# A streaming-encoder block on one core: the order of the two input norms' pieces in the engines' queues

## Chip, cores, metric

The kernel runs on 1 core of one Trainium2 chip. The metric is the device time of one execution in microseconds. A program on one core keeps five engines busy side by side: TensorE (PE, matmuls; PEld is its weight load), VectorE (DVE), ScalarE (ACT), GpSimd (POOL) and SyncE (SP, here only transfers). Each works off its own queue in order; an instruction that waits holds back everything behind it on its engine.

## The reference, cut to what matters

One layer on 512 tokens, with 16 learned meta tokens put in front (528 rows of 1024). The layer norms the rows, projects them to all branches at once, runs stick-breaking attention and gated linear attention, gates and adds both, adds the normed result to the input, and applies a gated MLP with a causal convolution, again normed on both sides:

```python
def _rmsnorm(x, g):
    xf = x.astype(jnp.float32)
    y = xf * lax.rsqrt(jnp.mean(xf * xf, axis=-1, keepdims=True) + EPS)
    return (y * g.astype(jnp.float32)).astype(x.dtype)

h = jnp.concatenate([meta, x], axis=1)
...
    hn = _rmsnorm(h, norm_mix_pre[l])            # the first norm
    proj = hn_p @ w_in[l]
    sb_q, sb_k, sb_v, g_q, g_k, g_v, g_r, g_lr, merge = _split_cols(proj, IN_WIDTHS)
    ...                                          # the two attention branches
    mix = (gate_sb * (sb @ w_sb_out[l]) + gate_gla * (o @ w_gla_out[l])) @ w_o[l]
    h = h + _rmsnorm(mix, norm_mix_post[l])      # the second norm: this one,
    hn = _rmsnorm(h, norm_ffn_pre[l])            # and this one behind it
    up = hn @ w_ffn_up[l]
    act = jax.nn.gelu(_causal_dwconv(up, conv_w[l], conv_b[l]), approximate=True)
    ffn = (act * (hn @ w_ffn_gate[l])) @ w_ffn_down[l]
    h = h + _rmsnorm(ffn, norm_ffn_post[l])
return h[:, N_META:]
```

## The kernel before

All matmul operands are split in two: a high part, the value rounded to a shorter format (a cast on ScalarE), and a low part, the rest (a subtraction on VectorE or GpSimd). A product is three matmuls: high by high, high by low, low by high. `load_w` (L79) loads a weight block `raw`, casts it to `wh` and subtracts to `wl`; `proj` (L100) runs the matmuls of one block of 128 output columns over up to two segments of tokens, `ALL` = 0 to 272 (meta tokens and tiles 1 and 2) and 272 to 528 (tiles 3 and 4). With `by_part` it takes all high-by-high matmuls first, then those with `wl`, then those with the input's low part.

**The order of the queues.** The kernel is traced as a sequence of operations, and a planner puts each engine's instructions in an order of its own: it simulates the program, and an engine takes what is ready by the simulated times, earlier-traced work first. A block under `with tc.issue_after(ins)` binds its instructions on the engine of `ins` behind `ins`. A tile with one buffer (`bufs=1`) is handed on only when its last reader is done, so instructions that write such tiles follow each other.

**First norm** (pool `p0`, L214 on). Four tiles of 128 tokens, `xts[1..4]`, and the meta tokens as one 128x128 tile `xm`. `stats(i)` squares and sums a tile on ScalarE and calls `rstd_of`, which gets 1/sqrt as exp(-ln/2) on ScalarE and refines it in three small steps on VectorE (L127, L132, L136; the last gives the factor). `scaled` applies the factor, `turned(i, r)` transposes on TensorE (`tp`, or `tpm` for the meta tokens) and calls `split_g`: gain on VectorE (`yg`, L210), cast to `hnh` on ScalarE (L211), low part `hnl` on the engine in the table `LO` (L212). The trace order is: tiles 1 and 2, the weights of the first block `gk` (columns C_GK) with its low part on VectorE, the loads of tiles 3 and 4, the meta tokens, some warming matmuls (`warm`), and the first half of the gk projection (`only=[0]`, tokens 0 to 272). Then come tiles 3 and 4, two rank-16 projections `lr` (L393), and in `gla_proj` the second half of gk.

**Second norm** (pool `pw`, L848 on). `second(i)` is the output projection of tile i for the right 512 columns (`wob`), `first_half(i, ...)` for the left (`wo`). `gained(i, pt, hf)` squares a half on ScalarE (`wj`, L863) and applies the gain on VectorE (`hb`, L864). `normed(i)` takes the factor over both halves (`whole`, L868), adds the input (L881), squares each half of the sum on ScalarE (`wk`, L883), takes the next factor and writes `y` (L888). `turned(i, b)` transposes half of y (`ht`, L897), casts it to `h2h` on ScalarE and subtracts to `h2l` on VectorE (L142, L143). The two meta tokens that the convolution needs go through `mini`, in three parts. All squares write one scratch tile `junk` with one buffer; the tiles of `rstd_of` have one buffer in this pool, too. The first two blocks of the MLP's up and gate projections (`up`, `ga`) are run for tiles 1 and 2 first, with the transposes of tiles 3 and 4 in between, and then for tiles 3, 4 and the meta columns.

Of the kernel before, what the change touches and what calls it, by code (L numbers as in the profile page):

```python
# [16 lines left out]
P = 128  # L17
# [32 lines left out]
def block_kernel(ctx: ExitStack, tc: tile.TileContext, x, meta_tokens, norm_mix_pre, w_in, w_gk_up, b_gk,  # L50
# [28 lines left out]
    def load_w(src, nk, name, hi_out=None, lo_out=None, lo_eng=pool, into=None):  # L79

        ncol = src.shape[-1]
        raw = wp.tile([P, nk, ncol], F32, tag="raw", name=f"raw_{name}")
        sp.dma_start(raw, src)
        last_raw[0] = raw
        if hi_out is None:
            hi_out = (into or wp).tile([P, nk, ncol], F32R, tag="wh", name=f"wh_{name}", bufs=2)
            lo_out = (into or wp).tile([P, nk, ncol], F32R, tag="wl", name=f"wl_{name}", bufs=2)
        act.copy(hi_out, raw)  # L88
        lo_eng.tensor_tensor(out=lo_out, in0=raw, in1=f32(hi_out), op=ALU.subtract)  # L89
        return hi_out, lo_out  # L90
# [26 lines left out]

    last_exp = [None]

    def rstd_of(pl, ss, n, name, between=None, rest=None):  # L120

        shp = list(ss.shape)
        r0 = pl.tile(shp, F32, tag=f"rs_r{shp[1]}", name=f"r0_{name}")
        act.activation(r0, ss, AF.Ln, scale=1.0 / n, bias=rest[0] if rest else epst[: shp[0]])
        last_exp[0] = act.activation(r0, r0, AF.Exp, scale=-0.5)
        v = pl.tile(shp, F32, tag=f"rs_v{shp[1]}", name=f"v_{name}")
        dve.tensor_scalar(out=v, in0=ss, scalar1=-0.5 / n, scalar2=rest[1] if rest else -0.5 * EPS, op0=ALU.mult, op1=ALU.add)  # L127
        if between:
            between()
        a = pl.tile(shp, F32, tag=f"rs_a{shp[1]}", name=f"a_{name}")  # L130
        if shp[1] == 1:
            dve.tensor_scalar(out=a, in0=v, scalar1=r0, scalar2=r0, op0=ALU.mult, op1=ALU.mult)  # L132
        else:
            dve.tensor_tensor(out=a, in0=r0, in1=r0, op=ALU.mult)
            dve.tensor_tensor(out=a, in0=a, in1=v, op=ALU.mult)
        dve.scalar_tensor_tensor(out=a, in0=a, scalar=1.5, in1=r0, op0=ALU.add, op1=ALU.mult)  # L136
        return a
# [69 lines left out]
    def split_g(pl, hi, lo, src, g, nm, lo_eng=dve):  # L207

        y = pl.tile([P, *src.shape[1:]], F32, tag="yg", name=f"yg{nm}", bufs=4)
        last_yg[0] = dve.tensor_tensor(out=y, in0=src, in1=g.unsqueeze(2).broadcast_to(list(src.shape)), op=ALU.mult)  # L210
        last_hi[0] = act.copy(hi, y)  # L211
        return lo_eng.tensor_tensor(out=lo, in0=y, in1=f32(hi), op=ALU.subtract)  # L212

    with tc.tile_pool(name="p0", bufs=2, side="right") as p0:  # L214
# [37 lines left out]
        def scaled(xt, r, eng):  # L252

            if eng is act:
                act.mul(xt, xt, r)
            else:
                eng.tensor_scalar(out=xt, in0=xt, scalar1=r, scalar2=None, op0=ALU.mult)

        def turned(i, r):
            if not i:  # L260
                tp = pst("tpm")
                last_tp[0] = pe.transpose(tp[:, :P], xm, ident)
                split_g(p0, hnh[:, :, :NM], hnl[:, :, :NM], tp[:, :P].rearrange("p (t k) -> p k t", k=KT), gT, "m")
                return
            t = slice(NM + (i - 1) * P, NM + i * P)
            for b in range(2):
                scaled(xts[i][:, 512 * b : 512 * b + 512], r, SC[i][b])
            for b in range(2):
                tp = pst(f"tp{i}_{b}", "sz"[i % 2])
                for k in range(4):  # L270
                    c = (4 * b + k) * P
                    with tc.issue_after(last_pr[0].ins) if i > 2 else ExitStack():
                        last_tp[0] = pe.transpose(tp[:, k * P : (k + 1) * P], xts[i][:, c : c + P], ident)
                ks = slice(4 * b, 4 * b + 4)
                low = split_g(p0, hnh[:, ks, t], hnl[:, ks, t], tp.rearrange("p (k t) -> p k t", k=4), gT[:, ks], f"{i}_{b}", LO[i][b])
            return low

        last_tp = [None]
        SC = {1: (dve, dve), 2: (act, dve), 3: (dve, dve), 4: (act, act)}
        LO = {1: (pool, pool), 2: (dve, pool), 3: (dve, pool), 4: (dve, pool)}  # L280
        d1 = stats(1)
        d2 = stats(2, last_exp[0])
        turned(1, d1)
        d0 = stats(0, last_exp[0])
        scaled(xm, d0, act)
        low2 = turned(2, d2)
        with tc.issue_after(last_exp[0].ins), tc.issue_after(last_yg[0].ins):
            first = {"k": load_w(cols(w_in, C_GK), KT, "gk0", lo_eng=dve)}
        for i in (3, 4):
            sp.dma_start(xts[i], x[(i - 1) * P : i * P, :])  # L290
        rlr = cst.tile([P, KT, RANK], F32, name="rlr")
        sp.dma_start(rlr, cols(w_in, C_LR, RANK))
        turned(0, d0)
        hi2 = last_hi[0]
        with tc.issue_after(last_tp[0].ins):
# [3 lines left out]
        d4 = stats(4, last_exp[0])  # L299
        turned(3, d3)  # L300
        low4 = turned(4, d4)

# [42 lines left out]
    with ExitStack() as pgs:  # L345
# [22 lines left out]
        with tc.tile_pool(name="plr", bufs=2) as plr:  # L368
# [20 lines left out]
            for lo, hi in ALL:  # L389
# [4 lines left out]
                if not lo:  # L394
                    first["lr"] = last_lr
                act.copy(gst[0:RANK, lo:hi], lr[0:RANK])
                act.copy(gst[64 : 64 + RANK, lo:hi], lr[0:RANK])
# [13 lines left out]
        def gla_proj(h):  # L411
            r = []
            for nm, c0, sc in (("k", C_GK + h * P, 1.0), ("q", C_GQ + h * P, GK ** -0.5)):
                w = first[nm] if h == 0 else load_w(cols(w_in, c0), KT, f"g{nm}{h}")
                if h == 0 and nm == "k":
                    pt = first["pt"]
                    proj(w, hnh, hnl, ALL, f"g{nm}{h}", only=[1], pt=pt)
                    pt = pt[:, 512 - 272 : 768]
# [429 lines left out]
    with tc.tile_pool(name="pw", bufs=1) as pw:  # L848
# [7 lines left out]
        sq2 = pw.tile([P, 5, 2], F32, name="sq2")  # L856

        def gained(i, pt, hf):
# [4 lines left out]
            act.activation(junk, pt, AF.Square, accum_out=sq[:, i, hf : hf + 1])  # L863
            dve.tensor_tensor(out=hb[:, i - 1, c], in0=pt, in1=g1bc[:, c], op=ALU.mult)  # L864
# [5 lines left out]

        last_tr = [None]

        ys = {}

        def normed(i):

            h, xi = hb[:, i - 1, :], xr[:, i - 1, :]
            r = whole(i, sq, "mix")
            for hf in range(2):
                c = slice(hf * 512, hf * 512 + 512)  # L880
                dve.scalar_tensor_tensor(out=h[:, c], in0=h[:, c], scalar=r, in1=xi[:, c], op0=ALU.mult, op1=ALU.add)  # L881
                junk = pw.tile([P, 512], F32, tag="junk", name=f"wk{i}_{hf}")
                act.activation(junk, h[:, c], AF.Square, accum_out=sq2[:, i, hf : hf + 1])  # L883
            r = whole(i, sq2, "ffn")
# [5 lines left out]
        def turned(i, b):  # L890
# [7 lines left out]
            ks = slice(4 * b, 4 * b + 4)  # L898
            split(h2h[:, ks, t], h2l[:, ks, t], tp.rearrange("p (k t) -> p k t", k=4))
            last_tr[0] = last_ht  # L900
# [90 lines left out]
        gained(3, second(3, {11: lambda: turned(1, 0), 17: lambda: turned(1, 1)}), 1)  # L991
        normed(3)
        m = mini()
        next(m)
        gained(4, second(4, {5: lambda: turned(2, 0), 11: lambda: turned(2, 1), 17: lambda: next(m)}), 1)
        normed(4)
        gas = [load_w(cols(w_gate, m * P), KT, f"ga{m}", into=wx) for m in range(2)]
# [264 lines left out]
```

## Time and profile before

| | |
|---|---|
| median of 3 runs | 939.47 us (938.93 to 939.78) |
| profiled execution | 938.61 us, of which the span of its instructions 936.9 us |
| busy in the span | PE 915.9 us (98%), PEld 839.4, DVE 621.9 (66%), ACT 494.2 (53%), POOL 355.6 (38%) |
| granted TensorE clock, mean | 0.992 |
| DMA | 93.38 MB, mean 100 GB/s |

Rows of instructions in order of time read: start in the span, duration of the group, engine, line of the kernel, operation, written tile <- read tiles, shape, count; in brackets the engine's idle time ahead of it and what ended it. Rows of a stretch give its length, the busy time of each engine with its number of instructions, the granted clock, and the DMA share and rate. Small groups of the same kind are merged into one row.

### The profile page before, as it was taken

The page shows a single profiled execution, that of the slowest core. Times are in us where ns is not written, and L with a number is a line of the kernel's source. Part 1 is how long each engine was busy: PE and PEld are TensorE (multiplying, and loading weights), DVE is VectorE, ACT ScalarE, POOL GpSimd, SP SyncE. Part 2 cuts the span into 40 slices and gives each one's busy share as a digit, 9 for nine tenths or more (in the row PEclk, how much of TensorE's full clock was granted, in tenths as well). Part 3 has the DMA queues.
Part 4 walks back from the last instruction along what each step waited for, and adds up shares of the span by engine and source line. Part 5 has one row for each costly group of instructions (what it writes and reads, how often), then busy time and mean ns, then how long its engine had stood idle before and what let it go on. Part 6 is the DMA issues. An engine that isn't in the chain of part 4 may idle for free.

```text
span 936.9 us, 17749 instructions
## 1 busy us (share of the span) xinstructions
PE 915.9 (98%) x7156; PEld 839.4 (90%) x7156; DVE 621.9 (66%) x1072; ACT 494.2 (53%) x938; POOL 355.6 (38%) x259
## 2 busy tenths in 40 slices
PE   7999999999999999999999998999999999999997
PEld 7999999999999998989998687999999999988885
DVE  6585858686559786888647357455554444578997
ACT  7674747575567665766754245433333333355654
POOL 6533332323355453555545322544444444200200
PEclk9999999999999999999999998999999999999999
DMA  7222222222222222222224542333333333264933
GB/s 203 66 70 75 63 68 69 69 69 69 69 68 69 68 66 72 68 69 68 57 79 127 211 135 90 108 96 91 90 91 90 93 100 100 91 232 184 239 113 131
DMA packets 129875, 93.38 MB, mean 100 GB/s; under 512 B 4080, under 2 KB 114930, under 8 KB 129794
## 3 DMA queue, kind: packets, MB, share of 16 engines
q1 hardware_dynamic: 126178, 82.55, 29.6%
q10 hardware_dynamic: 2112, 6.82, 1.9%
q0 software_dynamic: 1504, 2.88, 1.8%
q8 instruction: 56, 0.92, 0.4%
q14 instruction: 25, 0.20, 0.1%
HBM read 88.05 MB, written 4.19 MB: 98 GB/s over the span
## 4 chain that ended last, share of the span: by engine, by line
PE 94%; DVE 2%; ACT 2%; issue 1%; DMA 0%; POOL 0%; DVEq 0%; POOLq 0%; ACTq 0%
PE pt_up L115 14%; PE ga L936 13%; PE pt_gr L115 5%; PE pt_gv L115 5%; PE pt_mg L115 5%; PE pt_ms L115 5%; PE pt_go L115 5%; PE dA L1108 3%; PE dB L1108 3%; PE dD L1108 3%; PE pt_sv L115 3%; PE pt_gk L115 3%; PE pt_so L115 3%; PE wob L951 3%; PE pt_sk L115 3%; PE pt_gq L115 2%
## 5 line engine op out<-in xcount | busy, mean ns | idle before, releaser
L89 POOL TENSOR_TENSOR wl_up<-raw_up,wh_up 128x1024 fp32r<-128x1024 f32 x22 | 52.9, 2407 | 82.4 <-ACT wh_up L88 82.4
L89 POOL TENSOR_TENSOR wl_ga<-raw_ga,wh_ga 128x1024 fp32r<-128x1024 f32 x22 | 55.3, 2518 | 74.8 <-ACT wh_ga L88 57.5
L115 PE MATMUL pt_up<-h2h,wh_up 128*128 128x256 f32 (+1 forms) x352 | 74.7, 287 | 1.3 <-ACT h2h L142 1.3
L115 PE MATMUL pt_up<-h2l,wh_up 128*128 128x256 f32 (+1 forms) x352 | 74.6, 286 | 0.0
L115 PE MATMUL pt_up<-h2h,wl_up 128*128 128x256 f32 (+1 forms) x352 | 74.4, 285 | 0.0
L936 PE MATMUL ga<-h2h,wh_ga 128*128 128x512 f32 (+1 forms) x192 | 72.5, 377 | 0.0
L936 PE MATMUL ga<-h2h,wl_ga 128*128 128x512 f32 (+1 forms) x192 | 72.3, 377 | 0.0
L936 PE MATMUL ga<-h2l,wh_ga 128*128 128x512 f32 (+1 forms) x192 | 72.3, 377 | 0.0
L88 ACT CAST wh_up<-raw_up 128x1024 fp32r<-128x1024 f32 x22 | 23.1, 1049 | 79.3 <-PE pt_up L115 76.4
L115 PEld LDWEIGHTS pt_up<-h2h,wh_up 128*128 128x128 f32 x352 | 58.0, 193 | 3.5 <-ACT h2h L142 1.8
L115 PEld LDWEIGHTS pt_up<-h2l,wh_up 128*128 128x128 f32 x352 | 56.6, 193 | 0.0
L115 PEld LDWEIGHTS pt_up<-h2h,wl_up 128*128 128x128 f32 x352 | 56.5, 192 | 0.0
L936 PEld LDWEIGHTS ga<-h2h,wl_ga 128*128 128x128 f32 x192 | 36.4, 190 | 7.0
L936 PEld LDWEIGHTS ga<-h2h,wh_ga 128*128 128x128 f32 x192 | 36.7, 191 | 6.1
L936 PEld LDWEIGHTS ga<-h2l,wh_ga 128*128 128x128 f32 x192 | 36.4, 190 | 6.2
L1039 DVE SCALAR_TENSOR_TENSOR cy<-pt_up,cw,cy 128x511 f32<-128x511 f32 (+1 forms) x22 | 16.4, 745 | 36.7 <-ACT cy L1036 36.7
L88 ACT CAST wh_ga<-raw_ga 128x1024 fp32r<-128x1024 f32 x22 | 23.1, 1048 | 26.8 <-PE ga L936 25.6
L1039 DVE SCALAR_TENSOR_TENSOR yp<-pt_up,cw,yp 128x511 f32<-128x511 f32 (+1 forms) x22 | 16.4, 745 | 30.9 <-ACT yp L1036 30.9
L1136 POOL DMA_DIRECT2D tv<-in_w_ffn_down_dram x6 | 7.0, 1172 | 68.4 <-DVE wl_p L143 68.4
L89 POOL TENSOR_TENSOR wl_gr<-raw_gr,wh_gr 128x1024 fp32r<-128x1024 f32 x8 | 19.1, 2385 | 31.0 <-ACT wh_gr L88 29.5
L142 ACT CAST sh_p<-As 128x512 fp32r<-128x512 f32 (+1 forms) x30 | 17.3, 584 | 23.9 <-PE dB L1108 9.6
L115 PE MATMUL pt_gr<-hnh,wh_gr 128*128 128x258 f32 (+1 forms) x128 | 28.2, 294 | 0.0
(574 smaller groups left out, 3140.9 us busy)
## 6 DMA issues: line engine op xcount, KB each, us to landing
raw_up<-in_w_ffn_up_dram SPq DMA_DIRECT2D x22, 512.0 KB, 3.9
raw_ga<-in_w_ffn_gate_dram SPq DMA_DIRECT2D x22, 512.0 KB, 3.8
raw_t<-in_w_ffn_down_dram SPq DMA_DIRECT2D x10, 512.0 KB, 7.4
raw_gv<-in_w_in_dram SPq DMA_DIRECT2D x8, 512.0 KB, 3.9
raw_gr<-in_w_in_dram SPq DMA_DIRECT2D x8, 512.0 KB, 3.8
raw_mg<-in_w_in_dram SPq DMA_DIRECT2D x8, 512.0 KB, 3.9
raw_go<-in_w_gla_out_dram SPq DMA_DIRECT2D x8, 512.0 KB, 4.2
raw_ms<-in_w_in_dram SPq DMA_DIRECT2D x8, 512.0 KB, 3.8
```

What stands on the lines that cost most here:

```text
L88: act.copy(hi_out, raw)
L89: lo_eng.tensor_tensor(out=lo_out, in0=raw, in1=f32(hi_out), op=ALU.subtract)
L115: last_pr[0] = pe.matmul(dst, a[:, k, :], b[:, k, lo:hi], start=n == 0, stop=n == len(steps) - 1)
L142: act.copy(hi, src)
L936: last_mm[0] = pe.matmul(pt[:, lo:hi], a[:, k, :], b[:, k, lo:hi], start=lo == 0 and k == 0 and q == 0, stop=k == KT - 1 and q == 2, skip_ ...
L951: last_mm[0] = pe.matmul(pt, a, b, start=q == 0, stop=q == len(ops) - 1)
L1039: dve.scalar_tensor_tensor(out=y[:, d:], in0=pt[:, : SEQ - d], scalar=c, in1=y[:, d:], op0=ALU.mult, op1=ALU.add)
L1108: mm[i] = pe.matmul(dsts[i], a, b, start=first and k == 0 and j == 0, stop=last and k == NP - 1 and j == 2, skip_group_check=True)
L1136: return lambda n, q, nk: pool.dma_start(out=t[:, q : q + nk, :], in_=block(s, c, q, nk), accum_op=ALU.add)
```

## The change

In the first norm the order of the trace and the bindings are changed. `turned` only scales and transposes; `split_g` and the table move to `parted`. The gain of tile 2's second half is bound behind the meta tokens' factor `r0`; the casts of tile 1's second half and of tile 2 are bound behind the scaling of `xm`. The low parts of tile 1's second half and tile 2 and of the meta tokens all run on VectorE, behind the low part of gk's weights and one behind the other; before, GpSimd had both of tile 1 and the second of tile 2. The transpose of the meta tokens takes a buffer of the other PSUM tag. The loads of tiles 3 and 4 come after that in the trace. The second half of the gk projection moves to directly behind the first `lr` product, in the order of `by_part`.

In the second norm the first factors of tiles 3 and 4 are taken together, after tile 4's first square and ahead of both `normed`; tile 3's second squares are bound behind tile 4's first, and the casts of tile 3's transposes behind tile 4's last square.

```diff
@@ load_w, split_g: lo_eng=None leaves the low part to the caller
+        if lo_eng is None:
+            return raw, hi_out, lo_out
...
+        if lo_eng is None:
+            return lambda: dve.tensor_tensor(out=lo, in0=y, in1=f32(hi), op=ALU.subtract)
@@ first norm
-        LO = {1: (pool, pool), 2: (dve, pool), 3: (dve, pool), 4: (dve, pool)}
+        LO = {1: (pool, None), 2: (None, None), 3: (dve, pool), 4: (dve, pool)}
+        first = {}
         d1 = stats(1)
         d2 = stats(2, last_exp[0])
-        turned(1, d1)
+        t1 = turned(1, d1)
+        parted(1, 0, t1[0])
         d0 = stats(0, last_exp[0])
-        scaled(xm, d0, act)
-        low2 = turned(2, d2)
-        with tc.issue_after(last_exp[0].ins), tc.issue_after(last_yg[0].ins):
-            first = {"k": load_w(cols(w_in, C_GK), KT, "gk0", lo_eng=dve)}
+        r0 = last_r[0]
+        t2 = turned(2, d2)
+        with tc.issue_after(last_exp[0].ins):
+            raw, *first["k"] = load_w(cols(w_in, C_GK), KT, "gk0", lo_eng=None)
+        xs = scaled(xm, d0, act)
+        tp = pst("tpm", "z")
+        last_tp[0] = pe.transpose(tp[:, :P], xm, ident)
+        with tc.issue_after(xs.ins):
+            low11 = parted(1, 1, t1[1])
+        with tc.issue_after(xs.ins):
+            low20 = parted(2, 0, t2[0])
+        with tc.issue_after(r0.ins):
+            low21 = parted(2, 1, t2[1])
+        with tc.issue_after(last_yg[0].ins):
+            lowm = split_g(p0, hnh[:, :, :NM], hnl[:, :, :NM], tp[:, :P].rearrange("p (t k) -> p k t", k=KT), gT, "m", None)
+        hi2 = last_hi[0]
+
+        with tc.issue_after(last_yg[0].ins):
+            low = dve.tensor_tensor(out=first["k"][1], in0=raw, in1=f32(first["k"][0]), op=ALU.subtract)
+        with tc.issue_after(low.ins):
+            last = low20()
+        for f in (lowm, low11, low21):
+            with tc.issue_after(last.ins):
+                last = f()
         for i in (3, 4):
             sp.dma_start(xts[i], x[(i - 1) * P : i * P, :])
...
-        turned(0, d0)
-        hi2 = last_hi[0]
@@ rank projections and gla_proj
                 if not lo:
                     first["lr"] = last_lr
+                    proj(first["k"], hnh, hnl, ALL, "gk0", only=[1], pt=first["pt"], by_part=True)
...
-                    proj(w, hnh, hnl, ALL, f"g{nm}{h}", only=[1], pt=pt)
@@ second norm
-            act.activation(junk, pt, AF.Square, accum_out=sq[:, i, hf : hf + 1])
+            last_wj[0] = act.activation(junk, pt, AF.Square, accum_out=sq[:, i, hf : hf + 1])
...
-                act.activation(junk, h[:, c], AF.Square, accum_out=sq2[:, i, hf : hf + 1])
+                with tc.issue_after(last_wj[0].ins) if i == 3 else ExitStack():
+                    last_wk[0] = act.activation(junk, h[:, c], AF.Square, accum_out=sq2[:, i, hf : hf + 1])
...
-            split(h2h[:, ks, t], h2l[:, ks, t], tp.rearrange("p (k t) -> p k t", k=4))
+            with tc.issue_after(last_wk[0].ins) if i == 3 else ExitStack():
+                split(h2h[:, ks, t], h2l[:, ks, t], tp.rearrange("p (k t) -> p k t", k=4))
...
-        normed(3)
         m = mini()
         next(m)
         gained(4, second(4, {5: lambda: turned(2, 0), 11: lambda: turned(2, 1), 17: lambda: next(m)}), 1)
-        normed(4)
+        rs = [whole(i, sq, "mix") for i in (3, 4)]
+        normed(3, rs[0])
+        normed(4, rs[1])
```

More of the change, by code (lines that the diff above doesn't have):

```diff
@@ L118, in block_kernel @@
     last_exp = [None]
+    last_r = [None]
     def rstd_of(pl, ss, n, name, between=None, rest=None):
@@ L135, in rstd_of @@
             dve.tensor_tensor(out=a, in0=a, in1=v, op=ALU.mult)
-        dve.scalar_tensor_tensor(out=a, in0=a, scalar=1.5, in1=r0, op0=ALU.add, op1=ALU.mult)
+        last_r[0] = dve.scalar_tensor_tensor(out=a, in0=a, scalar=1.5, in1=r0, op0=ALU.add, op1=ALU.mult)
         return a
@@ L254, in scaled @@
             if eng is act:
-                act.mul(xt, xt, r)
-            else:
-                eng.tensor_scalar(out=xt, in0=xt, scalar1=r, scalar2=None, op0=ALU.mult)
+                return act.mul(xt, xt, r)
+            return eng.tensor_scalar(out=xt, in0=xt, scalar1=r, scalar2=None, op0=ALU.mult)
         def turned(i, r):
[L260 to L265, printed above, removed]
             for b in range(2):
                 scaled(xts[i][:, 512 * b : 512 * b + 512], r, SC[i][b])
+            tps = []
             for b in range(2):
-                tp = pst(f"tp{i}_{b}", "sz"[i % 2])
+                tps.append(pst(f"tp{i}_{b}", "sz"[i % 2]))
                 for k in range(4):
@@ L272, in turned @@
                     with tc.issue_after(last_pr[0].ins) if i > 2 else ExitStack():
[L273 to L276, printed above, removed]
+                        last_tp[0] = pe.transpose(tps[b][:, k * P : (k + 1) * P], xts[i][:, c : c + P], ident)
@@ L278, in block_kernel, with parted @@
+            return tps
+        def parted(i, b, tp):
+            t, ks = slice(NM + (i - 1) * P, NM + i * P), slice(4 * b, 4 * b + 4)
+            return split_g(p0, hnh[:, ks, t], hnl[:, ks, t], tp.rearrange("p (k t) -> p k t", k=4), gT[:, ks], f"{i}_{b}", LO[i][b])
         last_tp = [None]
         SC = {1: (dve, dve), 2: (act, dve), 3: (dve, dve), 4: (act, act)}
-        LO = {1: (pool, pool), 2: (dve, pool), 3: (dve, pool), 4: (dve, pool)}
+        LO = {1: (pool, None), 2: (None, None), 3: (dve, pool), 4: (dve, pool)}
@@ L299, in block_kernel @@
         d4 = stats(4, last_exp[0])
-        turned(3, d3)
-        low4 = turned(4, d4)
+        for i, d in ((3, d3), (4, d4)):
+            for b, tp in enumerate(turned(i, d)):
+                low4 = parted(i, b, tp)
         cr = p0.tile([FT, 4, P], F32, name="cr", bufs=1)
@@ L856, in block_kernel @@
         sq2 = pw.tile([P, 5, 2], F32, name="sq2")
+        last_wj = [None]
         def gained(i, pt, hf):
@@ L871, in block_kernel, with normed @@
         last_tr = [None]
+        last_wk = [None]
         ys = {}
-        def normed(i):
+        def normed(i, r=None):
             h, xi = hb[:, i - 1, :], xr[:, i - 1, :]
-            r = whole(i, sq, "mix")
+            r = whole(i, sq, "mix") if r is None else r
             for hf in range(2):
```

## The prediction, made before the run

> **What bounds the kernel now.** I read the shares by engine first, then the chain that ended last, then TensorE's waits, then the granted clock in stretches, and last the instructions in order of time around the two norms.
>
> ```profile
> PE 94%; DVE 2%; ACT 2%; issue 1%; DMA 0%; POOL 0%; DVEq 0%; POOLq 0%; ACTq 0%
> ```
>
> The chain is TensorE nearly throughout. So a change pays only where TensorE stands idle or slow, and what it saves there moves everything behind it. TensorE's waits name the places; the longest (total, times, longest) lies in the second norm, and one of 2.24 in the first (in brackets behind tpm, further down):
>
> ```profile
> PE ht L897 <- DVE y L888: 2.6, 1, 2.6
> ```
>
> A wait has an aftermath. The next rows are stretches of 3.41 us; their columns are length, busy PE, PEld, DVE, ACT, POOL, then the granted clock:
>
> ```profile
> 13.96:17.37 3.41, 3.41 (x17) 3.38 (x16) 2.23 (x7) 2.71 (x7) 1.54 (x1) 0.50 0.98 237
> 249.48:252.89 3.41, 3.41 (x20) 3.34 (x19) 0.12 (x1) 1.74 (x7) 2.29 (x1) 0.50 0.01 2
> 563.51:566.92 3.41, 1.86 (x14) 1.57 (x14) 2.68 (x4) 2.42 (x5) 3.41 (x2) 1.00 0.20 58
> 566.92:570.33 3.41, 3.41 (x19) 3.41 (x18) 3.31 (x13) 1.72 (x6) 0.31 (x1) 0.50 0.88 247
> 583.99:587.40 3.41, 3.41 (x17) 3.41 (x18) 1.23 (x2) 0.54 (x1) 0.00 (x0) 0.50 0.03 5
> ```
>
> After a stretch in which TensorE stood 1.55 us (563.51: 3.41 - 1.86), the next 3.41 us ran at clock 0.50, though TensorE was busy throughout. At half the rate such a stretch costs 3.41/2 = 1.7 us. The four slow stretches start a multiple of 3.413 us apart (235.52 = 69 of them, 317.44 = 93, 17.07 = 5), so they lie on a grid in time.
>
> **First norm.** ScalarE, then VectorE, then GpSimd, then TensorE, each in order of time (start, duration, engine, line, what):
>
> ```profile
> 10.05 1.03 ACT L88 CAST wh_gk<-raw_gk 128x1024 fp32r<-128x1024 f32 x1
> 10.99 1.65 ACT L211 CAST hnh<-yg 128x512 fp32r<-128x512 f32 x3
> 12.55 0.40 ACT L255 ACTIVATE xm<-xm,a_in 128x128 f32<-128x128 f32 x1
> 14.60 0.30 ACT L211 CAST hnh<-ygm 128x128 fp32r<-128x128 f32 x1 [1.65 <-DVE ygm L210]
> ```
>
> ```profile
> 10.57 0.26 DVE L132 TENSOR_SCALAR a_in<-v_in,r_in 128x1 f32<-128x1 f32 x1
> 10.80 0.69 DVE L210 TENSOR_TENSOR yg<-tp,gT 128x512 f32<-128x512 f32 x1
> 11.40 0.15 DVE L136 SCALAR_TENSOR_TENSOR a_in<-a_in,r_in 128x1 f32<-128x1 f32 x1
> 11.47 1.22 DVE L89 TENSOR_TENSOR wl_gk<-raw_gk,wh_gk 128x1024 fp32r<-128x1024 f32 x1
> 12.61 1.76 DVE L212 TENSOR_TENSOR hnl<-yg,hnh 128x512 fp32r<-128x512 f32 x1
> 14.29 0.28 DVE L210 TENSOR_TENSOR ygm<-tpm,gT 128x128 f32<-128x128 f32 x1
> ```
>
> ```profile
> 11.68 3.82 POOL L212 TENSOR_TENSOR hnl<-yg,hnh 128x512 fp32r<-128x512 f32 x2 [0.28 <-ACT hnh L211]
> ```
>
> ```profile
> 13.00 0.33 PE L262 MATMUL tpm<-ident,xm 128*128 128x128 f32 x1 [2.24 <-ACT xm L255]
> 13.16 2.05 PE L228 MATMUL warm<-ident 128*128 128x128 f32 x12
> 14.95 2.18 PE L115 MATMUL pt_gk<-hnh,wh_gk 128*128 128x272 f32 x8
> 16.93 1.36 PE L115 MATMUL pt_gk<-hnh,wl_gk 128*128 128x272 f32 x8
> 18.13 0.41 PE L115 MATMUL pt_gk<-hnl,wh_gk 128*128 128x272 f32 x2
> ```
>
> The first projection starts at 14.95, and the meta tokens set that: their factor is split by a gain of tile 2 (10.80 between 10.57 and 11.40), their scaling waits behind three casts (10.99 to 12.55), and their gain waits behind a low part that takes 1.76 while GpSimd subtracts too.
>
> After the change, step by step. (1) The gain at 10.80 is bound behind the factor, which then ends at 10.57 + 0.26 + 0.15 = about 11.02. (2) The three casts are bound behind the scaling, which starts when wh_gk ends (11.08) and ends at 11.48. (3) The transpose starts at 11.55, the twelve warming matmuls behind it; in the row 14.95 - 13.00 = 1.95 us pass from transpose to projection, so the projection can start at 13.50. (4) VectorE: the moved gain runs 11.05 to 11.74, ygm 12.0 to 12.3. (5) ScalarE: the three casts 11.48 to 13.1, the meta cast to 13.4, in time for 13.50. The gain is 14.95 - 13.50 = 1.45 us.
>
> What is moved lands on VectorE: low parts of tile 1's and tile 2's second halves leave GpSimd, and wl_gk now waits for ygm, with four low parts in a fixed order behind it. GpSimd keeps one subtraction, ahead of them, so I price a 512-wide low part at 0.69, not 1.76, from this later row:
>
> ```profile
> 26.32 0.69 DVE L212 TENSOR_TENSOR hnl<-yg,hnh 128x512 fp32r<-128x512 f32 x1
> ```
>
> From 12.3: 1.22 + 3 x 0.69 + 0.3 (128 wide, as ygm) = 15.9. wl_gk is there at 13.5 and first wanted 1.98 us after the start (16.93 - 14.95), at 15.5; the low parts 3.18 us after it (18.13 - 14.95), at 16.7. So they are hidden with 0.8 to spare at the slow clock. Without that cover (a fast clock wants them at 13.50 + 16 x 0.125 = 15.5) they cost 0.4. If they ran at 1.76 each they would end at 19.1 and cost 2.4: the bounds are 0 and 2.4, and I take 0, since the row of a VectorE alone is the near one. Tiles 3 and 4 follow the last meta cast through ScalarE, which starts their squares as much sooner. SP's transfers keep their order, but now stand in the trace behind the casts of gk; those for tiles 3 and 4 wait for no result, and I count nothing.
>
> The second half of the gk projection is moved ahead, between the two rank projections, and taken in the order high, low weight, low input. TensorE does the same matmuls, so the price is 0 unless it then meets a low part that is not there (the 26.32 row is the last of them): between a loss of 2.2 us and no effect; I take 0.
>
> **Second norm.** ScalarE, VectorE, TensorE:
>
> ```profile
> 571.17 0.60 ACT L863 ACTIVATE wj<-wob 128x512 f32<-128x512 f32 x1
> ...
> 575.88 0.63 ACT L883 ACTIVATE wk<-hb 128x512 f32<-128x512 f32 x1 [2.23 <-DVE hb L881]
> 576.42 0.18 ACT L883 ACTIVATION_READ_ACCUMULATOR wk<-hb 128x1 f32 x1
> 578.13 0.59 ACT L142 CAST h2h<-ht 128x512 fp32r<-128x512 f32 x1 [1.53 <-PE ht L897]
> 578.14 0.33 ACTq L1009 DMA_DIRECT2D hbd<-hb  x1
> 578.62 0.63 ACT L883 ACTIVATE wk<-hb 128x512 f32<-128x512 f32 x1
> ```
>
> ```profile
> 574.59 0.28 DVE L132 TENSOR_SCALAR a_mix<-v_mix,r_mix 128x1 f32<-128x1 f32 x1
> 574.90 0.16 DVE L136 SCALAR_TENSOR_TENSOR a_mix<-a_mix,r_mix 128x1 f32<-128x1 f32 x1
> 575.09 1.41 DVE L881 SCALAR_TENSOR_TENSOR hb<-hb,a_mix,xr 128x512 f32<-128x512 f32 x2
> ...
> 581.71 1.41 DVE L888 SCALAR_TENSOR_TENSOR y<-hb,a_ffn,g2bc 128x512 f32<-128x512 f32 x2
> 583.04 0.17 DVE L143 TENSOR_TENSOR h2l<-hmg,h2h 128x16 fp32r<-128x16 f32 x1
> ```
>
> ```profile
> 582.52 1.38 PE L897 MATMUL ht<-ident,y 128*128 128x128 f32 x8 [2.56 <-DVE y L888]
> ```
>
> The last tile's second half was ready at 576.5 (575.09 + 1.41), but its square stood behind a cast that waited 1.53 for a transpose, and ran at 578.62. y followed at 581.71, and TensorE stood 2.56. The change binds that cast behind the square: 2.1 us (578.62 - 576.5) by itself. It also takes tile 4's first square (571.17) ahead of tile 3's second ones, and both first factors ahead of both tiles. The factor's tile has one buffer, so tile 4's factor still waits until tile 3's hb is done; but it no longer waits for tile 3's y. y moves by the stretch between: a y pair (1.41) and the two or three small steps around it (0.28, 0.16 each), some 2 us more. Of 4.1 us TensorE needs 2.56. So the wait goes, and the slow stretch after it (1.7) has no cause.
>
> What is late next: TensorE goes from the transposes straight to the second halves, which need the casts of tile 4 (0.59 each) and the meta columns, whose low part came at 583.04, behind y. With y gone from there I take 0.3 us of new waiting; the bounds are 0 and 2.56 (all of it given back). In front, tile 4's first square (0.60) may now stand before a cast of tile 2, which TensorE waits for (part of the 1.55 in the stretch from 563.51): 0 to 0.6, and I take 0, since the casts come first in the trace. Gain: 2.56 + 1.7 - 0.3 = 3.96 us.
>
> The Trainium skill, "TensorE: Matmul & The Clock Gate", section "HAM oscillation — how this bites in real kernels", gives as its rule that gaps above about 3.4 us are to be avoided. The trace differs: 1.55 us in one stretch was enough. By that rule a gap of 2.56 would leave the clock alone, and the sum would lose its 1.7. The same page (Part 1) says the window is free-running and does not reset with the kernel; the grid of 3.413 agrees, and no run here shows whether its phase repeats.
>
> **Sum.** 1.45 + 3.96 = 5.4 us. The profiled execution took 938.61 (span 936.9 and 1.7 around it), 0.86 under the median of 939.47. 938.61 - 5.4 = 933.2, beside that median 934.1.
>
> **Rivals.**
> *More slow stretches go.* The gap in front of the first projection shrinks by 1.45, and the others shift on the grid; 249.48 and 566.92 follow gaps only just long enough to slow a stretch. Against: in the first norm tiles 3 and 4 are then bound by ScalarE, which gains no more than 1.45. Two stretches: 934.1 - 3.4 = 930.7.
> *Another wait takes its place.* The meta columns or the casts of tile 4 hold the second halves for more than 1.5 us, and the stretch after it stays slow: 934.1 + 1.2 + 1.7 = 937.0. For: 583.04 is later than TensorE would come. Against: what held it there was y.
> *The slow stretch has another cause than the gap* (the page's rule, for one): 934.1 + 1.7 = 935.8. Against: 563.51 and 566.92.
> *The change does not do what it says*: the queues are planned from the trace order, and a plan that leaves the meta tokens and the square where they are gives 939.5.
> *Slower.* The moved second half of gk stands in TensorE's queue ahead of the gq matmuls, and the last low part of tile 4 (26.32) is planned still later on VectorE. From the chain in order of time, the first rank projection:
>
> ```profile
> 21.19 2.00 PE lr L393 x16
> ```
>
> It would end at 21.7 (1.45 sooner), and 16 matmuls of gk at the same 2.00/16 = 0.125 bring TensorE to the low parts at 23.7. Waiting W there costs W and a slow stretch of 1.7; slower by 0.2% (1.9 us, about what a measurement of this kernel can tell) begins at W = 5.4 + 1.9 - 1.7 = 5.6, that is, a low part at 29.3. At W = 6 the time is 934.1 + 7.7 = 941.8. Against: the row has it at 27.01, and its inputs come sooner now.
>
> **How the numbers follow.** Forecast 0.50, more stretches 0.14, another wait 0.12, other cause 0.07, no effect 0.11, slower 0.06. The first four are faster by over 0.2% (below 937.6): 0.83; same 0.11; slower 0.06. The range runs from 930.7 to 937.6, which leaves out the last two (0.17); the forecast's own range is 932.4 (a third stretch gone) to 935.8.
>
> **What would show it.** Right: pt_gk begins near 13.5; the low parts of tiles 1 and 2 take 0.69 on VectorE; L863 runs four times ahead of tile 3's L883; ht's wait on y is gone, and the clock is 1.00 over the stretches behind it. Wrong: a wait of lr or gk on hnl between 20 and 27, of pt_up on h2h after the last transposes, or slow stretches at new places.

## The result

The changed kernel takes 932.16 us (931.42 to 934.14) beside 939.55 us for the one before: a ratio of 0.9928, 95% interval 0.9913 to 0.9943. Timed again beside the experiments it took 932.68 us, ratio 0.9935 (0.9918 to 0.9952). The forecast was 934.1 in a range from 930.7 to 937.6. The total fell where the prediction put it; the experiments show that two of its steps do not hold, and that a part of the total is chance. One execution among the experiments (of the move of gk alone) took 1260.4 us at a mean clock of 0.653 and is left out of its ratio.

The profiled execution took 931.42 us, with a span of 929.7 (before: 936.9) at a mean granted clock of 0.999. The shares of the chain, and TensorE's longest waits around the change:

```profile
PE 91%; DVE 4%; ACT 2%; SPq 1%; issue 1%; DMA 0%; POOL 0%; DVEq 0%; POOLq 0%; ACTq 0%
```

```profile
PE pt_up L117 <- ACT h2h L145: 1.3, 1, 1.3
PE tpm L295 <- ACT xm L260: 1.1, 1, 1.1
PE ga L965 <- ACT h2h L145: 0.7, 1, 0.7
```

The wait of `ht` on `y` (2.56) is gone; 0.68 for a cast of tile 4 came in its place. The first norm's wait halved. Stretches on the 3.41 us grid of this profile, near those that ran slow before:

```profile
13.29:16.70 3.41, 3.33 (x27) 3.14 (x26) 3.20 (x10) 3.31 (x9) 0.00 (x0) 1.00 0.98 258
248.81:252.22 3.41, 3.41 (x32) 3.39 (x31) 1.28 (x5) 1.53 (x6) 2.64 (x3) 1.00 0.05 15
566.25:569.66 3.41, 3.41 (x31) 3.41 (x30) 3.37 (x14) 2.27 (x8) 0.00 (x0) 1.00 0.72 235
579.90:583.31 3.41, 3.41 (x31) 3.41 (x30) 0.30 (x1) 0.00 (x0) 0.00 (x0) 1.00 0.00 0
```

All four are at full clock; the forecast's sum had only the last one (583.99) gone. What one costs is read from the start of the same matmuls in both profiles. TensorE's lead over the kernel before grows from 1.07 us (`zs`, 247.16 to 246.09) to 2.60 (`pt_mg`, 256.07 to 253.47) across the stretch at 249, and from 2.57 (`pt_up`, 564.92 to 562.35) to 4.09 (a `ga` matmul, 572.61 to 568.52) across the one at 567: 1.5 us each.

The first norm, VectorE, ScalarE and TensorE:

```profile
10.99 0.55 DVE L139 SCALAR_TENSOR_TENSOR a_in<-a_in,r_in 128x1 f32<-128x1 f32 x1
...
12.67 1.22 DVE L307 TENSOR_TENSOR wl_gk<-raw_gk,wh_gk 128x1024 fp32r<-128x1024 f32 x1
13.80 0.68 DVE L216 TENSOR_TENSOR hnl<-yg,hnh 128x512 fp32r<-128x512 f32 x1
...
14.60 1.29 DVE L216 TENSOR_TENSOR hnl<-yg,hnh 128x512 fp32r<-128x512 f32 x2
```

```profile
11.57 0.40 ACT L260 ACTIVATE xm<-xm,a_in 128x128 f32<-128x128 f32 x1 [0.36 <-DVE a_in L139]
11.87 1.64 ACT L214 CAST hnh<-yg 128x512 fp32r<-128x512 f32 x3
```

```profile
12.02 0.33 PE L295 MATMUL tpm<-ident,xm 128*128 128x128 f32 x1 [1.14 <-ACT xm L260]
13.77 1.27 PE L117 MATMUL pt_gk<-hnh,wh_gk 128*128 128x272 f32 x8
15.88 1.16 PE L117 MATMUL pt_gk<-hnl,wh_gk 128*128 128x272 f32 x8
18.75 0.29 PE L416 MATMUL lr<-hnh,wst 128*48 128x272 f32 x1 [0.44 <-DVE yg L213]
```

The scaling of `xm` runs ahead of the three casts, the low parts are in the bound order at 0.65 to 0.68 each, and the first projection starts at 13.77 instead of 14.95. One thing the forecast did not have: the sum of squares of tile 3 is ready at 14.77, 1.2 us sooner than before, but VectorE takes it up at 15.81, behind the low parts, so tile 3's scaling starts only 0.39 sooner (17.05 to 16.66). TensorE then waits 0.44 for a gain. Whether another order would save this was not tried.

The second norm, ScalarE, VectorE, TensorE:

```profile
563.23 0.63 ACT L888 ACTIVATE wj<-wob 128x512 f32<-128x512 f32 x1
567.36 0.63 ACT L911 ACTIVATE wk<-hb 128x512 f32<-128x512 f32 x1 [0.26 <-DVE hb L907]
...
570.62 0.62 ACT L911 ACTIVATE wk<-hb 128x512 f32<-128x512 f32 x1
```

```profile
573.98 1.42 DVE L916 SCALAR_TENSOR_TENSOR y<-hb,a_ffn,g2bc 128x512 f32<-128x512 f32 x2
```

```profile
575.54 1.45 PE L925 MATMUL ht<-ident,y 128*128 128x128 f32 x8
577.66 0.50 PE L965 MATMUL ga<-h2h,wh_ga 128*128 128x256 f32 x2 [0.68 <-ACT h2h L145]
```

Tile 4's first square is ahead of tile 3's second ones, and tile 4's y starts 7.73 us sooner (581.71 to 573.98), of which 2.6 us were saved ahead of this norm (`pt_up` starts at 562.35 instead of 564.92).

Where the 7.2 us of the two spans went, by when TensorE starts a block in both traces: 1.1 by the stick-breaking projections (rows below), 2.6 by `pt_mg` (256.1 to 253.5), still 2.6 at `pt_up`, and 7.2 at its end (817.8 to 810.6). So: first norm 1.1, the stretch at 249 1.5, the second norm 4.6, which is the stretch at 567 (1.5), 1.9 of waiting (2.56 less 0.68) and, as the rest, 1.2 for the stretch behind the wait.

```profile
209.15 0.41 PE L115 MATMUL pt_sk<-hnh,wh_sk 128*128 128x272 f32 x2
```

```profile
208.05 0.41 PE L117 MATMUL pt_sk<-hnh,wh_sk 128*128 128x272 f32 x2
```

Not all of this belongs to the change. Of the 14 profiles of this case, the stretch near 249 is slow in five of the six with the old first norm and in none of the eight with the new one, so it goes with the first norm. A slow stretch follows the wait of 1.3 of `pt_up` in ten of the twelve profiles that have this wait, the changed kernel's second one among them, so its absence here is chance. That second profile has a span of 931.2: 5.7 us less than before instead of 7.2. Its `pt_sk` starts at 208.62, so the first norm gains only 0.5 there.

### The profile page after: what moved, and what is told of

It reads as the page before. It is cut to its first block, busy times and chain, and to the rows that moved or that the text cites. A ratio compares the mean times of both kernels' runs of the same rounds, so it can differ in the third digit from the quotient of the medians.

```text
span 929.7 us, 17750 instructions
## 1 busy us (share of the span) xinstructions
PE 910.6 (98%) x7156; PEld 833.6 (90%) x7156; DVE 620.6 (67%) x1074; ACT 493.9 (53%) x938; POOL 351.8 (38%) x257
## 4 chain that ended last, share of the span: by engine, by line
PE 91%; DVE 4%; ACT 2%; SPq 1%; issue 1%; DMA 0%; POOL 0%; DVEq 0%; POOLq 0%; ACTq 0%
PE pt_up L117 13%; PE ga L965 13%; PE pt_gr L117 5%; PE pt_gv L117 5%; PE pt_mg L117 5%; PE pt_ms L117 5%; PE pt_go L117 5%; PE dA L1138 3%; PE dB L1138 3%; PE dD L1138 3%; PE pt_sv L117 3%; PE pt_sk L117 3%; PE pt_gq L117 3%; PE wo L1001 2%; PE wob L980 2%; PE pt_gk L117 2%
```

## The experiments

Kernels told under one heading ran on one chip and share its runs of the kernel before. Kernels of different headings ran on different chips, so their ratios compare better than their times.

### The two norms apart, and the clock (before: 938.29)

**The kernel before, unchanged.**

> The kernel before, unchanged, for the mean granted clock of each of its runs. Theory: the 3.41 us stretches at half clock lie on a grid whose phase differs from run to run, so the number of slow stretches varies (mean clock 0.992 for four of them, about 0.002 more for each one fewer) and the time falls by 0.9 to 1.7 us for each one fewer. Rival: the grid starts with the kernel, every run has the same four, and the clock stays at 0.992.

937.75 us, ratio 1.0000 (0.9986 to 1.0013). Over these executions and those of the kernel before beside them the clock varies from 0.988 to 0.994; the 25 at 0.992 averaged 938.33, the 12 at 0.994 averaged 937.10. The clock is not the same in every execution, so the rival does not hold. One slow stretch is worth 0.0018 of mean clock (half of 3.41 over 937), so by these times it costs about 1.2 us, an estimate from two groups.

**The first norm's change alone** (with the move of gk):

```diff
-        rs = [whole(i, sq, "mix") for i in (3, 4)]
-        normed(3, rs[0]); normed(4, rs[1])
+        normed(3)      # ahead of tile 4's second(4), as before
+        ...
+        normed(4)      # and no issue_after for wk and h2h of tile 3
```

> The change in the first norm and in the gk projection alone; the second norm is as before. Theory (the first norm is worth its earlier start, and about 1.0 us of it is left at the first stick-breaking projection): first gk matmul near 13.8, first pt_sk matmul near 208.1, the 2.6 us wait of ht on y stays; 0.8 to 2.7 us faster than before, the more the fewer slow stretches fall in. Rival (the first norm's shift alone took the slow stretches at 249 and 567 away): 4 us faster or more.

932.63 us, ratio 0.9943 (0.9929 to 0.9958). The rival's figure was met, its reason in part: the stretch at 249 is at full clock here, but one at 563.15 is slow. The larger part neither named: the wait of `ht` on `y` went without the edit that was to take it away. ScalarE and TensorE:

```profile
573.21 0.63 ACT L909 ACTIVATE wk<-hb 128x512 f32<-128x512 f32 x1 [2.22 <-DVE hb L907]
573.84 0.57 ACT L145 CAST h2h<-ht 128x512 fp32r<-128x512 f32 x1
574.31 0.63 ACT L909 ACTIVATE wk<-hb 128x512 f32<-128x512 f32 x1
```

```profile
573.07 0.60 PE L923 MATMUL ht<-ident,y 128*128 128x128 f32 x4
```

The planner, given another first norm, put tile 3's first transposes 15 TensorE rows closer behind `msmix` (69 rows between them instead of 84). They were done when ScalarE came to their cast, which waited for nothing, and tile 4's second square followed at once.

**The second norm's change alone:**

```diff
+        rs = [whole(i, sq, "mix") for i in (3, 4)]
+        normed(3, rs[0]); normed(4, rs[1])   # with both issue_after; the first norm as before
```

> The change in the second norm alone; the first norm and the gk projection are as before. Theory: the 2.6 us wait becomes about 0.7 and the slow stretch behind it goes: first gk matmul at 14.95, 3 to 4.5 us faster than before. Rival (the second norm is worth only its wait, since the stretch behind it would be slow anyhow): 1.9 us faster.

936.12 us, ratio 0.9979 (0.9969 to 0.9989): 2.0 us, under the 3 to 4.5 expected, and the rival's figure without its reason. The 2.56 became three waits of 0.27, 0.35 and 0.68, and only the stretch behind them was spared. ScalarE:

```profile
574.89 0.20 ACT L125 ACTIVATE r_ffn<-r_ffn 128x1 f32<-128x1 f32 x1
579.31 0.59 ACT L142 CAST h2h<-ht 128x512 fp32r<-128x512 f32 x1 [4.22 <-PE ht L902]
```

Here tile 3's transposes are planned later (94 rows behind `msmix`), and their casts stand idle for them. By the ratios the two parts alone give 5.3 and 2.0 us, and the whole change 6.8, or 6.1 as timed again. So in the whole change the second norm's edit adds 0.8 to 1.4 us to the first norm's change, which the overlapping intervals do not tell from nothing.

**The kernel before, with its wait of 2.56 filled** by twenty matmuls that add zero:

```diff
+        with tc.issue_after(last_31.ins):
+            for _ in range(20):
+                pe.matmul(pgs_[1][:64, 0:256], nil, h2h[:, 0, 0:256], start=False, stop=False, ...)
```

> The kernel before, with 20 extra matmuls of a 128x64 tile of zeros put into the 2.6 us in which TensorE waits for y of the last tile (they add zero to an accumulator in use). The wait for y stays as long as it was, but TensorE is busy in it. Theory (the gap causes the slow stretch behind it): granted clock 1.00 in the 7 us behind the last transposes, 0.9 to 1.7 us faster than before. Rival (the slow stretch has another cause than the gap): still a stretch at 0.50 there, and the same time as before within 0.3 us.

937.71 us, ratio 0.9995 (0.9983 to 1.0008): no gain that the times show, though the interval has room for 1.6 us. The mean clock of the twelve executions is 0.992, as before. The profile does show a gain. TensorE, and the stretch behind the wait, first in the kernel before (unchanged), then in this one:

```profile
579.81 2.58 PE L1013 MATMUL ga<-h2h,nil 128*64 128x256 f32 x20
582.62 1.38 PE L897 MATMUL ht<-ident,y 128*128 128x128 f32 x8 [0.23 <-DVE y L888]
```

```profile
583.22:586.63 3.41, 3.31 (x17) 3.33 (x17) 1.44 (x3) 1.17 (x2) 0.00 (x0) 0.50 0.02 5
```

```profile
583.20:586.60 3.40, 3.30 (x25) 2.89 (x25) 1.49 (x4) 1.18 (x2) 0.00 (x0) 1.00 0.02 5
```

The first profile of the kernel before, whose grid lies within 0.1 us of this one's, has its slow stretch at 583.99; with the gap filled, no stretch is slow between 571 and 932. So in the profile the gap, not its place, slows the stretch. The spans differ by 1.0 to 1.2 (936.7 and 936.9 against 935.7): the prediction's 1.7 was too much, the more so here, where TensorE also waits for casts. That the twelve executions together show neither more clock nor less time stays open.

### The move of gk, the casts (before: 938.53)

**The changed kernel again.**

> The changed kernel unchanged, as the reference for the other kernels beside it. Every theory: 932.2 as in its first runs (931.4 to 934.1), 0.993 of the kernel before. What it tells apart is the slow stretches: if their places are chance, this profile has another number of them than the one tail stretch of the first; if the change fixes them, it has the same.

932.68 us. This profile has slow stretches at 11.60 and 564.56 where the first had none, and a span of 931.2 instead of 929.7. So their number is chance within one kernel: 1.5 us here.

**The second half of gk put back** behind both rank projections, the rest as changed:

```diff
-                    proj(first["k"], hnh, hnl, ALL, "gk0", only=[1], pt=first["pt"], by_part=True)
...
+                    proj(w, hnh, hnl, ALL, f"g{nm}{h}", only=[1], pt=pt)
```

> The changed kernel with one part undone: the second half of the first gk projection stands again behind both rank projections. Theory (the moved half makes the second rank projection 1.6 us later, so the log decays are late and the cumulative sums wait for them): the second rank projection starts 1.4 to 2 us sooner, the cumulative sums of the first heads end about 0.5 sooner, and the time is 0.3 to 0.8 us under the changed kernel's, 931.6. Rival (the move gives TensorE work while tile 4's low parts are made): TensorE waits for a low part of tile 4 and the kernel is up to 1 us slower, 933.2. The transposes of tile 3 in the second norm are planned some 10 matmuls later in this kernel than in the changed one's, as in the second norm alone; if that place does not matter, the second norm's wait stays at 0.7 to 1.3.

937.52 us, ratio 0.9988 (0.9978 to 0.9998): 4.8 us slower than the changed kernel. The theory fell outright; the wait that the rival named came, but cost more than its 1 us. VectorE, TensorE, and the stretches around:

```profile
24.08 2.55 DVE L405 CAST wg<-rwg 16x512 fp32r<-16x512 f32 x3
26.66 0.69 DVE L217 TENSOR_TENSOR hnl<-yg,hnh 128x512 fp32r<-128x512 f32 x1
```

```profile
25.60 0.28 PE L117 MATMUL pt_gq<-hnh,wh_gq 128*128 128x256 f32 x1
27.41 0.32 PE L416 MATMUL lr<-hnl,wst 128*48 128x256 f32 x1 [1.53 <-DVE hnl L217]
```

```profile
24.63:28.04 3.41, 1.88 (x19) 1.55 (x18) 3.30 (x5) 0.23 (x1) 2.95 (x5) 1.00 0.00 0
28.04:31.45 3.41, 3.41 (x19) 3.25 (x18) 0.75 (x7) 1.04 (x3) 1.46 (x3) 0.50 0.00 0
```

TensorE now wants tile 4's low part at 25.88, 1.2 us sooner than in the kernel before (27.12), but it ends at 27.35, 0.3 later than there, behind three casts of a small gate weight. TensorE waits 1.53 for it and then runs a stretch at half clock. `pt_sk` starts at 212.05, 4.0 us behind the changed kernel; the wait and a slow stretch of 1.5 make 3.0 of it, and the rest was not traced. Behind that, the second norm has tile 3's transposes at 94 rows here and waits 0.3 twice more. The moved half of gk is work that covers this: in the changed kernel it keeps TensorE busy up to the matmuls that need the low part (27.56), which has just ended:

```profile
27.56 1.10 PE L117 MATMUL pt_gk<-hnl,wh_gk 128*128 128x256 f32 x8
```

```profile
26.67 0.69 DVE L217 TENSOR_TENSOR hnl<-yg,hnh 128x512 fp32r<-128x512 f32 x1
```

**The second gate weight's cast bound behind tile 2's last cast**, the rest as changed:

```diff
+            with tc.issue_after(cast2.ins) if m_ else ExitStack():
+                gas.append(load_w(cols(w_gate, m_ * P), KT, f"ga{m_}", into=wx))
```

> The changed kernel, and the cast of the second gate weight (1.03 us on ScalarE) bound behind tile 2's last cast in the second norm. Theory (that cast stands ahead of the one that TensorE waits 1.3 for): the wait of pt_up on h2h falls from 1.3 to 0.5 or less and the kernel is 0.8 to 1 us faster than the changed one, 931.3. Rival (the square of tile 4's half, 0.60, takes its place ahead, or the gate weight now comes late for ga): the same time within 0.3, or a wait of ga on wh_ga of about 1 us and no gain.

932.01 us, ratio 0.9934 (0.9917 to 0.9952), as the changed kernel's 0.9935. TensorE's waits:

```profile
PE ht L927 <- DVE mssffn L950: 1.4, 1, 1.4
...
PE pt_up L117 <- ACT h2h L145: 0.4, 1, 0.4
```

The wait in front fell as expected, from 1.3 to 0.4, and was given back at tile 4: its y starts at 574.45 here, 0.47 later than in the changed kernel, although `pt_up` started 0.9 sooner. So by the ratios the rival's equal time held, for a reason that is neither of its two.

**One edit in the kernel before: only tile 3's casts bound behind the last square:**

```diff
+            with tc.issue_after(last_wk[0].ins) if i == 3 else ExitStack():
+                split(h2h[:, ks, t], h2l[:, ks, t], ...)
```

> The kernel before, and one edit alone: the cast of tile 3's transposes that waited 1.53 is bound behind the square of the last tile's second half. Prediction's step (this cast alone cost 2.1 us): the wait of 2.56 falls to about 0.5, the slow stretch behind it goes, and the kernel is 2 to 3.3 us faster than before, 935 to 936 beside 938.3. Rival (tile 3's transposes are planned too late, and the cast bound behind the square then holds up TensorE's next group, or the earlier squares were needed too): the wait stays above 1.2 and the gain is under 1.3.

939.62 us, ratio 1.0012 (1.0002 to 1.0021): nothing gained, and the wait stays at 2.6; the rival was right. ScalarE and VectorE:

```profile
577.08 0.63 ACT L884 ACTIVATE wk<-hb 128x512 f32<-128x512 f32 x1 [0.31 <-ACT wk L884]
...
580.15 0.59 ACT L142 CAST h2h<-ht 128x512 fp32r<-128x512 f32 x1 [0.90 <-PE ht L898]
580.63 0.30 ACT L125 ACTIVATE r_ffn<-r_ffn 128x2 f32<-128x2 f32 x2
```

```profile
581.94 1.41 DVE L889 SCALAR_TENSOR_TENSOR y<-hb,a_ffn,g2bc 128x512 f32<-128x512 f32 x2
```

The square came 1.54 sooner (578.62 to 577.08). The next cast in the queue then waited for its transposes, ahead of the second step of the root that y needs, and y came no sooner (581.94, before 581.71; TensorE runs 0.2 later in this profile).

### What the first norm's parts are worth (before: 938.64)

**The two second-half low parts back on GpSimd:**

```diff
-        LO = {1: (pool, None), 2: (None, None), 3: (dve, pool), 4: (dve, pool)}
+        LO = {1: (pool, pool), 2: (None, pool), 3: (dve, pool), 4: (dve, pool)}
-        for f in (lowm, low11, low21):
+        for f in (lowm,):
```

> The changed kernel with the second-half low parts of tiles 1 and 2 back on GpSimd; the meta tokens' order, the gk move and the second norm stay as changed. The prediction's step (a low part takes 1.76 where the two engines subtract together, 0.69 to 0.68 on VectorE alone) with TensorE wanting the low parts at 15.88: GpSimd has 10.24 to 11.51 for the first one, so the second would run from about 13.1 and the third to about 16.5, and VectorE's subtractions beside them grow from 0.68 to 1.2 or more; the first gk projection's low part waits 0.6 to 2, and the kernel is 0.5 to 2 us slower than the changed one, 933 to 934.5. Rival (the eight low-input matmuls take half of their operands from the first halves, which stay early): the same within 0.4, 932.4.

934.51 us, ratio 0.9965 (0.9952 to 0.9978): slower than the changed kernel (932.68, ratio 0.9935, on another chip) by 1.8 us in the medians and 2.8 in the ratios. VectorE, beside two subtractions on GpSimd from 12.47 to 15.98:

```profile
12.72 2.10 DVE L307 TENSOR_TENSOR wl_gk<-raw_gk,wh_gk 128x1024 fp32r<-128x1024 f32 x1
14.74 1.78 DVE L216 TENSOR_TENSOR hnl<-yg,hnh 128x512 fp32r<-128x512 f32 x1
```

VectorE's subtractions grew as expected (1.22 and 0.68 on VectorE alone), but the wait of the first gk projection for a low part, which was to cost 0.6 to 2, did not come. This profile and the changed kernel's second one have the same slow stretches, so their places compare: 0.5 us are lost in the first norm (`pt_sk` at 209.1, not 208.6) and 0.9 more in the second (`pt_up` ends at 813.4, not 812.0), where transposes wait 0.3 twice again, though nothing was edited there. The total is what was expected, its larger part from the reordered second norm: the step held in its durations and not in its price.

The Trainium skill, "SBUF — State Buffer", section "Who interferes with whom", says that a VectorE instruction with two SBUF inputs contends with a GpSimd instruction that reads SBUF, and one with a single SBUF input does not. These rows agree, as does the factor's step of 0.55, and so does a gain `yg`, whose other input lies in PSUM: in the kernel before it took 0.68 (from 9.97) while GpSimd subtracted (10.12 to 11.39).

**The move of gk alone, in the kernel before:**

```diff
+                    proj(first["k"], hnh, hnl, ALL, "gk0", only=[1], pt=first["pt"], by_part=True)
...
-                    proj(w, hnh, hnl, ALL, f"g{nm}{h}", only=[1], pt=pt)
```

> The kernel before, and one edit alone: the second half of the first gk projection is moved between the two rank projections. Theory (the moved half is only worth something because it covers the wait for tile 4's low part, and in the kernel before TensorE reaches the second rank projection at 27.12, when that low part has just ended at 27.01): no wait to cover, so no change, within 0.8 us of before, 937.7 to 938.5. Rival (the move is worth 4 us by itself, as it was with the meta tokens ahead): 934 to 935.

939.27 us, ratio 1.0003 (0.9991 to 1.0014): no change, as the theory had it (its range in time, up to 938.5, was missed by 0.8). The move is worth 4.8 us where TensorE comes early and nothing that the times show where it does not.

**gk put back, and tile 4's low part ahead of the small casts:**

```diff
-            with tc.issue_after(last_yg[0].ins):
+            with tc.issue_after(last_yg[0].ins), tc.issue_after(low40.ins):
                 for q in (0, 32, 96):
                     dve.tensor_copy(wg[q : q + RANK, :], rwg)
```

> The changed kernel with the second half of gk back behind both rank projections, and one more edit: on VectorE the casts of the small gate weight (2.55 us from 24.08) are bound behind tile 4's low part instead of standing ahead of it. Theory (the 5 us lost with the half put back came from that low part, ready at 27.35 where TensorE wanted it at 25.9, and from the slow stretch behind the wait of 1.53): the low part ends near 24.5, the wait and the slow stretch go, and the kernel is 3 to 5 us faster than with the half put back alone, 932 to 934.5. Rival (the place of the half itself matters, for the planned order of what follows): it stays at 936 to 937.5.

932.32 us, ratio 0.9938 (0.9922 to 0.9955): faster than with gk put back alone by 5.2 us in the medians and 4.7 in the ratios, as expected. VectorE and TensorE:

```profile
23.98 0.73 DVE L217 TENSOR_TENSOR hnl<-yg,hnh 128x512 fp32r<-128x512 f32 x1
24.63 2.64 DVE L407 CAST wg<-rwg 16x512 fp32r<-16x512 f32 x3
```

```profile
25.61 0.28 PE L418 MATMUL lr<-hnl,wst 128*48 128x256 f32 x1
```

The wait is gone at its root: the low part ends at 24.71, TensorE takes it at 25.61, and `pt_sk` starts at 207.56, 0.5 ahead of the changed kernel. So the late low part is the main cause, shown from both sides: covered by work, or made sooner. A smaller part may be order: tile 3's transposes are back at 84 rows here.

### A version with all of it (before: 938.52)

```diff
+        with tc.issue_after(last_tp[0].ins):
+            for _ in range(8):
+                pe.matmul(tp[:, :P], ident, ident, start=True, stop=True)   # ahead of xm's transpose
... gk put back, low part first, the late gate weight, and in normed(4):
+                    with tc.issue_after(last_red[0].ins):   # the reduction to mssffn
+                        dve.scalar_tensor_tensor(out=y[:, c], ...)
```

> A candidate beyond the changed kernel. To the kernel with the half of gk put back and tile 4's low part first it adds three edits: the second gate weight's cast behind tile 2's last cast, tile 4's y behind the reduction of the meta tokens' second sum of squares, and eight warming matmuls ahead of the meta tokens' transpose, in the idle time there. Theory (each is one wait or one slow stretch: 0.5 for the log decays, which came 0.5 sooner with the low part first; the 1.3 wait of pt_up on h2h is under 0.5; the wait of ht on mssffn that took its place falls from 1.4 to 0.7; no slow stretch behind the first norm or behind the 1.3 wait): 930.6 to 931.5, 0.7 to 1.6 under the changed kernel. Rival (what is saved in front is waited for at tile 4's y, whose chain on VectorE did not move): 931.8 to 932.4, as the changed kernel.

933.71 us, ratio 0.9945 (0.9926 to 0.9963): not better than the changed kernel, and above both ranges that were expected. TensorE:

```profile
10.96 2.81 PE L298 MATMUL tpm<-ident 128*128 128x128 f32 x16
13.60 0.27 PE L299 MATMUL tpm<-ident,xm 128*128 128x128 f32 x1
```

The filler was too long. Its eight matmuls are sixteen instructions in the trace; they ran partly at half clock (a slow stretch starts at 9.32), and held the meta tokens' transpose until 13.60 (12.02 in the changed kernel). In the second norm the 1.4 of `ht` went, and 1.3 came for another operand (`h2l`). No version here beats the changed kernel clearly.

## Why the prediction was right, and where it was not

**The total** was right, in part by luck: 5.4 us forecast, 6.8 measured by the ratio (6.1 timed again), 7.2 between the profiles. The terms of the sum came to 4.2 there: 1.1 for the first norm, 1.9 of waiting, 1.2 for the stretch behind it, where the forecast had 1.45, 2.26 and 1.7. The rest is the first rival, two more slow stretches at 1.5 each. The one at 249 goes with the first norm's change; the other holds in some executions and not in others.

**First norm, 1.45.** The projection's start moved by 1.18. The factor's last step took 0.55 beside a GpSimd subtraction, not 0.15, the first tile's transfer was 0.12 late, and 1.75 instead of 1.95 passed between transpose and projection. The low parts were hidden from this projection, as priced.

**The move of gk, priced at 0** with a loss of 2.2 at the other end, is the step that failed. A gain was left out of its bounds. The prediction had half of what decides it: the low part of tile 4 ended at 27.01. The other half is when TensorE took it in the kernel before:

```profile
27.12 0.28 PE L393 MATMUL lr<-hnl,wst 128*48 128x256 f32 x1
```

With a slack of 0.1, the 1.2 us that TensorE gained up to this place could only be waited off, unless something else was put in between. That no wait came in the changed kernel is luck by the prediction's own figures: with TensorE at the low parts at 23.7 and the row at 27.01 they give a wait of 3.3, and 0 was taken all the same. The estimate of 23.7 left out 25 matmuls of gq and 8 of `cwt`, which stand in between in both kernels; TensorE came at 27.56. The sentence that tiles 3 and 4 are "bound by ScalarE" looked at the wrong engine here: it was VectorE's queue, with 2.55 us of small casts ahead. Without the move the first norm's change is worth nothing that can be told: 0.9988 with gk put back, 0.9979 for the second norm alone.

**The cast that "cost 2.1 us by itself"** was the other failed step. The edit alone gives nothing (1.0012), since the next cast takes over the wait. All edits of the second norm together move y more than priced: it follows the start of `pt_up` by 11.6 us instead of 16.8, in the changed kernel and with the second norm alone, which is 5.2 where 4.1 was forecast. What TensorE gains by it depends on when it runs tile 3's transposes. At 84 rows behind `msmix`, as before, the wait goes with all edits (changed kernel) and stays with the cast alone; at 69 rows it goes without any (first norm alone); at 94 rows a part comes back in spite of them (second norm alone). The place differs from 84 in six of the 14 profiles, in three of them (first norm alone, gk put back, low parts on GpSimd) although the second norm is that of a kernel with 84. Which of the planner's simulated times does it was not tried.

**The slow stretch, 1.7.** That the gap is its cause is shown in one profile (the filled wait), and the pattern over all profiles agrees; the times do not show it. Its size is 1.5 where TensorE has work throughout (the lead of one profile over the other), 1.0 to 1.3 behind the last transposes, 1.2 by the times. The Trainium skill's rule in "TensorE: Matmul & The Clock Gate", section "HAM oscillation — how this bites in real kernels" (gaps above some 3.4 us), is not what these runs show: between 7 and 900 us, all 24 stretches of the 14 profiles with 1.53 us or more of idle time were followed by a slow one, none of them with more than 2.61.

**Another wait takes its place** happened in small: 0.68 for the casts of tile 4, where 0.3 was taken. **Slower** did not: no low part was missed, but with 27.36 against 27.56 it was closer than the prediction's "its inputs come sooner now" has it.

## What to carry to other kernels

Before moving an operation forward, look up the next thing that its consumer will want and by how much it is early; a slack of 0.1 us downstream turned a gain of 1.2 us upstream into a wait here, until that operand is made sooner or other work is put in front of it. Ending one wait in a queue hands it to the next instruction that waits for the same producer, so price the whole queue up to the instruction that counts. And where a planner orders the queues, an edit's effect includes every place that it reorders: run the halves apart before crediting either, and tell what goes with the change from what one profile shows by chance.

## What the hardware showed that was not expected

Slow stretches lie on a grid of 3.413 us in every profile, but the grid's phase against the kernel's start differs from run to run: modulo 3.413 it was 3.05 and 1.36 in the two profiles of the changed kernel. The Trainium skill, "TensorE: Matmul & The Clock Gate", Part 1, has the window free-running, and this agrees. So the same gap slows the next stretch in one execution and not in another, as the grid cuts it or not: around the wait of `pt_up` in the changed kernel, at most 1.33 us of idle time fell into one stretch in the first profile and 1.56 in the second. Idle time is not the whole rule. A stretch with 1.11 us of it near 246 was followed by a slow one in five profiles and not in a sixth, 1.38 near 406 in none, and at the kernel's end, where no matmuls follow, five stretches with 1.58 to 1.88 were not followed by one, two with 1.97 and 2.97 were. What else counts stays open. A step on one element for each partition (128x1) took 0.55 us instead of 0.15 beside a GpSimd subtraction: small instructions are held up as well.
